# Sums of the activation blocks right behind their transposes, and act transposed on VectorE and through memory, in a hybrid decoder layer

## The chip, the cores and the metric

The kernel runs on one core of a Trainium2 chip. The metric is the device time of one execution in microseconds (us). The engines are named as in the profile: PE (TensorE, matrix products), PEld (its weight loads), DVE (VectorE), ACT (ScalarE), POOL (GpSimd), SP (SyncE, which issues nearly all transfers). SBUF is the on-chip memory, PSUM the banks that PE writes to.

## What is computed

One decoder layer in float32, 256 tokens, width 2048, inner width 5632 of the feed-forward part. The change touches the second half alone: the end of the mixer, the norm behind it and the feed-forward part. Cut to that, with the mixer's output as `mix`:

```python
mix = jnp.einsum('bse,ed->bsd', mix, w_out[l])
x = x + rmsnorm(mix, norm_post_mix[l])
h = rmsnorm(x, norm_pre_ffn[l])
g = jnp.einsum('bsd,df->bsf', h, w_gate[l])
up = jnp.einsum('bsd,df->bsf', h, w_up[l])
f = jnp.einsum('bsf,fd->bsd', jax.nn.silu(g) * up, w_down[l])
x = x + rmsnorm(f, norm_post_ffn[l])
```

## The kernel before

Every product is made of three passes: an operand is split into a rounded part h and a rest l, and PE sums h·h, l·h and h·l. ACT casts a weight tile w (128x2048) to wh (L185, for the pairs below L920), DVE forms wl = w − wh (L186, L921).

The program's order is written out by hand. A list holds steps, each of 12 matmuls on 128x512, for one of two blocks of 128 tokens (tb=0, 1). At each step the stream first resumes the side jobs whose time has come (`yield n` in a job means: go on n steps later), then splits the weight tile four places ahead, issues the next loads on SP as slots come free (three for w, two for raw), and then writes the step's matmuls. Each engine runs its instructions in that order. One instruction that waits holds up all behind it on its engine, and SP likewise.

The mixer's last chunk ends in `residual(tb)` (L747-802): it makes x, transposes it on PE, and writes H2, the split operand of gate and up. For tb=1 it ends with `form_sums` (L726) and `split_sums` (L741), the sums and differences S of H2's blocks that the pairs need.

The feed-forward part runs over 11 column blocks f of 512, in four parts: f=0-2, 3-5, 6-8, 9-10. f=0 has a plain chunk for gate and one for up (`post_gate` L822, `post_up` L831). Every later f is a `Pair`, which computes half of gate and up by seven products over sums of blocks (s1 to s7) and the rest plainly (g0, g1, u0, u1); the steps of u0 and u1 of f fill in between those of the pair of f+1, or in front of the down chunks when f ends a part:

```python
return (s[1] + fill[0] + s[7] + s[6] + fill[1] + s[5] + s[2] + s[3] + g[0] + g[1] + s[4])
```

s7 accumulates in the bank b7, which the pair before frees with its gate add for tb=1 (`gate`, L1006). Behind s5, ACT copies the bank to s (L1023) and s3 waits for this copy.

When u1 of f is done, sg holds act, tokens on partitions. `act_put` (L1037; for f=0 the end of `post_up`) turns it, 8 PE transposes of 128x128 into PSUM (tile ft), from where ACT casts h (L208) and DVE subtracts l (L209) into the tile act, the operand of the down products. After each part the down chunks n=0-3 run (L1079-1094): for each n, over the part's k tiles (one for each f), two steps each; a step on the k of f needs act of f.

Tiles named M come from a pool of three buffers of 128x1024: sg, v, s and others share it.

Of the kernel before, what the change touches and what calls it, by code (L numbers as in the profile page):

```python
# [25 lines left out]
F32 = mybir.dt.float32  # L26
# [34 lines left out]
def hybrid_layer_kernel(ctx: ExitStack, tc: tile.TileContext, x, xt, pack, lamv,  # L61
# [25 lines left out]
    def v3(ap, n):  # L87
        return ap.rearrange("p (a b) -> p a b", a=n)
# [637 lines left out]
    def form_sums():  # L726

        r = v3(T("sums"), 4)
        h, l = H2.part(1)
        for tb in range(2):  # L730
            tok = slice(tb * P, (tb + 1) * P)

            nc.vector.tensor_tensor(out=r[:, 2 * tb:2 * tb + 2].rearrange("p a (k t) -> p (a k) t", k=4),
                                    in0=h[:, :, tok].bitcast(F32), in1=l[:, :, tok].bitcast(F32),
                                    op=ALU.add)
        for o, a, b, op in [(3, 2, 3, ALU.add), (2, 0, 2, ALU.subtract), (0, 3, 0, ALU.subtract),
                            (1, 1, 0, ALU.subtract)]:
            nc.vector.tensor_tensor(out=r[:, o], in0=r[:, a], in1=r[:, b], op=op)
        return r

    def split_sums(r):  # L741
        sh, sl = v3(T("sumh", F32R), 4), v3(T("suml", F32R), 4)
        nc.scalar.copy(sh, r)
        nc.vector.tensor_tensor(out=sl, in0=r, in1=sh.bitcast(F32), op=ALU.subtract)
        st_["S"] = [t.rearrange("p s (k t) -> p s k t", k=4) for t in (sh, sl)]

    def residual(tb, bank):  # L747
        xr, mg = st_["x", tb], st_["mixg", tb]
        tok = slice(tb * P, (tb + 1) * P)
        square_into(bank, part[:, tb, 3:4])  # L750
        if tb:
            yield 1
        nc.vector.tensor_tensor(out=mg[:, 3 * C:], in0=bank, in1=st_["gpost"][:, 3 * C:],
                                op=ALU.mult)
        r = partial_rstd(part, tb, "rpost")

        def x2(n):
            c = slice(n * C, (n + 1) * C)
            nc.vector.scalar_tensor_tensor(out=xr[:, c], in0=mg[:, c], scalar=r[:, 0:1],
                                           in1=xr[:, c], op0=ALU.mult, op1=ALU.add)  # L760

        def tr(n):
            bk = aux_bank("ht")
            for j in range(4):
                nc.tensor.transpose(bk[:, j * P:(j + 1) * P],
                                    xr[:, n * C + j * P:n * C + (j + 1) * P], ident)
            for eng in range(2):
                for j in range(4):
                    k = n * 4 + j
                    g = pk[:, PK_GFFN + k:PK_GFFN + k + 1]  # L770
                    h, l = H2.at(k, 1, tok)
                    b = bk[:, j * P:(j + 1) * P]
                    if eng == 0:
                        nc.scalar.activation(h[:, 0], b, ACTF.Copy, scale=g)
                    else:
                        nc.vector.scalar_tensor_tensor(out=l[:, 0], in0=b, scalar=g,
                                                       in1=h[:, 0].bitcast(F32), op0=ALU.mult,
                                                       op1=ALU.subtract)

        x2(0)  # L780
        yield 1
        x2(1)
        x2(2)
        yield 1
        x2(3)
        tr(0)
        for n in range(1, 4):
            yield 1
            tr(n)
        yield 3  # L790
        for n in range(4):
            square_into(xr[:, n * C:(n + 1) * C], part2[:, tb, n:n + 1])
        yield 1
        rstd2[tb] = partial_rstd(part2, tb, "rffn")

        nc.sync.dma_start(xd[tb], xr)
        st_["x", tb] = None
        if tb:
            yield 1
            r = form_sums()  # L800
            yield 2
            split_sums(r)

    oc = []
    need = {0: [lambda: st_["av", 0]], 4: [lambda: st_["av", 1]],
# [16 lines left out]
    def post_gate(f, bank):  # L822
        while rstd2[0] is None or rstd2[1] is None:
            yield 1
        sg = v3(M("sg"), 2)
        st_["sg", f] = sg
        for tb in range(2):
            nc.scalar.activation(sg[:, tb], bank[tb], ACTF.Silu, scale=rstd2[tb][:, 0:1])
        st_["gate", f] = True

    def post_up(f, A, k, bank):  # L831
        while ("gate", f) not in st_:
            yield 1
        sg = st_["sg", f]
        for tb in range(2):
            nc.vector.scalar_tensor_tensor(out=sg[:, tb], in0=bank[tb], scalar=rstd2[tb][:, 0:1],
                                           in1=sg[:, tb], op0=ALU.mult, op1=ALU.mult)
            dve[0] += 0.6
        yield 2
        for tb in range(2):  # L840
            bk = aux_bank("ft")
            for j in range(4):
                nc.tensor.transpose(bk[:, j * P:(j + 1) * P], sg[:, tb, j * P:(j + 1) * P], ident)
            A.put_psum(k, 4, slice(tb * P, (tb + 1) * P), v3(bk, 4))

    def down_evac(pi, last, n, tb, bank):
        c = slice(n * C, (n + 1) * C)
# [39 lines left out]
    class Act:  # L887
# [9 lines left out]
            t = self.t[f]  # L897
            return t[:, 0, k % 4:k % 4 + n, tok], t[:, 1, k % 4:k % 4 + n, tok]

        put_psum = Operand.put_psum  # L900

    class Slot:

# [22 lines left out]
    class Pair:  # L926
# [88 lines left out]
        def after(self, what, tb):  # L1015
            if what == 1:
                self.v = v3(M("v"), 2)
                nc.scalar.copy(self.v[:, 0], self.b1)
            elif what == 6:
                nc.scalar.copy(self.v[:, 1], self.b1)  # L1020
            elif what == 5:
                self.s = M("s")[:, :C]
                nc.scalar.copy(self.s, self.b1)  # L1023
                nc.vector.tensor_tensor(out=self.s, in0=self.b7, in1=self.s, op=ALU.add)
            elif what == "g1" and tb == 0:
                self.sg = v3(M("sg"), 2)
                spawn(self.gate(0, self.b2, self.v[:, 0])).run()
            elif what == 4:
                spawn(self.gate(1, self.b7, self.v[:, 1])).run()
            elif what == "u1" and tb == 0:  # L1030
                self.up(0, self.b1)
            elif what == "u1":
                nc.vector.tensor_tensor(out=self.s, in0=self.b8, in1=self.s, op=ALU.add)
                self.up(1, self.s)
                st_["act", self.f] = spawn(act_put(self.A, self.k, self.sg), 3)

    def act_put(A, k, sg):  # L1037
        for tb in range(2):
            bk = aux_bank("ft")
            for j in range(4):  # L1040
                nc.tensor.transpose(bk[:, j * P:(j + 1) * P], sg[:, tb, j * P:(j + 1) * P], ident)  # L1041
            A.put_psum(k, 4, slice(tb * P, (tb + 1) * P), v3(bk, 4))
        yield 1

    def reload():
        load_gain(1, "gpf")
# [6 lines left out]
    for pi, (f0, f1) in enumerate(parts):  # L1053
        A = Act()
        last = pi == len(parts) - 1
        needs = {}
        for f in range(f0, f1):
            k = (f - f0) * 4
            needs[k] = [lambda f=f: st_["act", f]]
            if f:  # L1060
                pair = Pair(f, A, k)
                put(pair.steps(fill))
                fill = pair.up_steps()
                continue
            c = both(lambda bank, f=f: post_gate(f, bank))(Chunk("gate", H2))
            add(c, w_tiles(w_gate, 0, [(f * C, C)], 0, KT), stagger=True)

            def hook(bank, f=f, A=A, k=k):
                j = Job(post_up(f, A, k, bank), now[0])
                st_["act", f] = j  # L1070
                side.append(j)
            c = Chunk("up", H2)
            c.done = lambda tb, c=c, hook=hook: hook(c.bank) if c.left == [0, 0] else None
            st = steps_of(c, w_tiles(w_up, 0, [(f * C, C)], 0, KT))
            put(st[:4])
            fill = [st[4:6], st[6:]]
        put(fill[0] + fill[1])
        nk = (f1 - f0) * 4
        for n in range(4):  # L1079
            c = Chunk("down", A, needs=needs)  # L1080
            ts = w_tiles(w_down, f0 * C, [(n * C, C)], 0, nk)
            if last and n == 0:
                ts[0][1].post.append(reload)
            if last and n == 3:
                c.done = lambda tb, c=c, pi=pi: spawn(finish(pi, tb, c.bank[tb]))
                add(c, ts, stagger=True)
                continue
            both(lambda bank, pi=pi, last=last, n=n: post_down(pi, last, n, bank))(c)
            st = steps_of(c, ts)
            if n == 3:  # L1090
                put(st[:-4])
                fill = [st[-4:-2], st[-2:]]
            else:
                put(st)
# [82 lines left out]
```

## Time and profile before

| | |
|---|---|
| time, median of three runs | 1080.97 us (1080.56 to 1081.28) |
| the profiled execution: time, span | 1080.65 us, 1078.9 us |
| PE busy, share of the span, instructions | 1052.6 us, 98%, 4766 |
| DVE | 823.2 us, 76%, 858 |
| ACT | 562.4 us, 52%, 586 |
| transfers of queue q1: MB, share of 16 engines' span | 213.21 MB, 57.7% |
| the chain that ended last | PE 84%, DVE 8%, ACT 3%, DMA 2%, issue 2% |

The rows further down come from several views of one profiled execution. A busy PE isn't PE at its peak: the rows with PEclk give the clock that it was granted, 1.00 being 2.4 GHz and 0.50 being 1.2 GHz. A matmul's own duration (390 ns for 128x512) is longer than the distance from one to the next, since they overlap; a step of 12 takes 2.72 us from start to start. The idle time of an engine matters only where someone waits for it.

### The profile page before, as it was taken

To read this page: it belongs to the slowest core of one execution; us is meant where nothing else is said; L and a number is where in the kernel's file an instruction comes from. 1 tells how busy PE (TensorE), PEld (TensorE's weight loads), DVE (VectorE), ACT (ScalarE), POOL (GpSimd) and SP (SyncE) were. 2 spreads that over 40 slices of the span, in tenths; PEclk is the share of its full clock that TensorE was granted. 3 is DMA by queue.
4 is the path that set the end of the run, shared out by engine and by line. 5 is a ranking of instruction groups with operands and counts; after the bars stand their busy time and mean duration, and the time that the engine had idled before them with its cause. 6 is when DMAs were issued, how large, how long until landed. Compare 5 with 4: busy or idle time off the path is not lost.

```text
span 1078.9 us, 12015 instructions
## 1 busy us (share of the span) xinstructions
PE 1052.6 (98%) x4766; PEld 866.3 (80%) x4766; DVE 823.2 (76%) x858; ACT 562.4 (52%) x586; POOL 10.8 (1%) x16
## 2 busy tenths in 40 slices
PE   9999999999999979999999999999999999999986
PEld 7778888888888858888888887888888788888865
DVE  6589989898656888875578987567898855789655
ACT  6764564655645654654454655335465533446441
POOL 0000000001000000000000000000000000000000
PEclk9999999999999989999999999999999999999989
DMA  9876555444766627277354827745473684453922
GB/s 309 291 271 197 193 157 195 156 156 156 271 199 233 199 105 279 78 273 262 128 195 156 294 97 256 257 150 195 156 255 121 231 290 156 154 197 131 354 100 78
DMA packets 114265, 213.97 MB, mean 198 GB/s; under 512 B 4089, under 2 KB 23841, under 8 KB 112929
## 3 DMA queue, kind: packets, MB, share of 16 engines
q1 hardware_dynamic: 114208, 213.21, 57.7%
q8 instruction: 37, 0.61, 0.2%
q14 instruction: 20, 0.16, 0.0%
HBM read 208.99 MB, written 4.21 MB: 198 GB/s over the span
## 4 chain that ended last, share of the span: by engine, by line
PE 84%; DVE 8%; ACT 3%; DMA 2%; issue 2%; POOL 1%; SPq 0%; DVEq 0%; POOLq 0%; ACTq 0%
PE b L999 23%; PE mm L259 15%; PE mm L260 15%; PE mm L262 15%; PE b L1002 11%; DVE wl L186 2%; DVE wl L921 2%; ACT wh L185 2%; DMA w<-in_w_in_dram 1%; DVE w L954 1%; PE ft L1041 1%; DVE conv_acc L442 1%; DMA rb<-in_rel_bias_dram 1%; ACT wh L920 1%; PE scmm L262 1%
## 5 line engine op out<-in xcount | busy, mean ns | idle before, releaser
L186 DVE TENSOR_TENSOR wl<-w,wh 128x2048 fp32r<-128x2048 f32 (+1 forms) x160 | 340.6, 2130 | 130.4 <-ACT wh L185 126.8
L185 ACT CAST wh<-w 128x2048 fp32r<-128x2048 f32 (+1 forms) x160 | 285.0, 1783 | 186.8 <-PE mm L260 92.8
L999 PE MATMUL b<-wh,h2h 128*128 128x512 f32 x440 | 171.9, 391 | 0.0
L1002 PE MATMUL b<-wh,h2l 128*128 128x512 f32 x440 | 171.3, 389 | 0.0
L259 PE MATMUL mm<-wh,act 128*128 128x512 f32 x352 | 138.5, 393 | 2.5 <-ACT act L208 2.5
L260 PE MATMUL mm<-wh,act 128*128 128x512 f32 x352 | 138.2, 393 | 1.6 <-DVE act L209 1.6
L259 PE MATMUL mm<-wh,xh 128*128 128x512 f32 x320 | 128.0, 400 | 0.9 <-ACT wh L185 0.9
L260 PE MATMUL mm<-wh,xl 128*128 128x512 f32 x320 | 125.2, 391 | 0.0
L921 DVE TENSOR_TENSOR wl<-w,wh 128x2048 fp32r<-128x2048 f32 x40 | 91.6, 2289 | 38.1 <-ACT wh L920 37.3
L999 PE MATMUL b<-wl,h2h 128*128 128x512 f32 x440 | 117.7, 389 | 0.0
L920 ACT CAST wh<-w 128x2048 fp32r<-128x2048 f32 x40 | 76.5, 1912 | 73.0 <-DVE w L954 42.6
L999 PEld LDWEIGHTS b<-wl,h2h 128*128 128x128 f32 x440 | 82.6, 188 | 17.2
L999 PEld LDWEIGHTS b<-wh,h2h 128*128 128x128 f32 x440 | 82.6, 188 | 17.0
L1002 PEld LDWEIGHTS b<-wh,h2l 128*128 128x128 f32 x440 | 82.7, 188 | 16.9
L262 PE MATMUL mm<-wl,act 128*128 128x512 f32 x352 | 94.6, 391 | 0.0
L442 DVE SCALAR_TENSOR_TENSOR conv_acc<-conv_in,pk,conv_acc 128x255 f32<-128x255 f32 (+14 forms) x240 | 94.4, 467 | 0.0
L921 DVE TENSOR_TENSOR wl<-raw,wh 128x2048 fp32r<-128x2048 f32 x30 | 68.2, 2290 | 26.0 <-ACT wh L920 26.0
L262 PE MATMUL mm<-wl,xh 128*128 128x512 f32 x320 | 87.4, 391 | 0.2 <-DVE wl L186 0.2
L920 ACT CAST wh<-raw 128x2048 fp32r<-128x2048 f32 x30 | 57.4, 1913 | 50.6 <-DVE raw L954 45.9
L259 PEld LDWEIGHTS mm<-wh,act 128*128 128x128 f32 x352 | 66.6, 189 | 16.4 <-ACT act L208 2.7
L260 PEld LDWEIGHTS mm<-wh,act 128*128 128x128 f32 x352 | 66.6, 189 | 15.9 <-DVE act L209 2.2
L262 PEld LDWEIGHTS mm<-wl,act 128*128 128x128 f32 x352 | 66.5, 189 | 14.0
(170 smaller groups left out, 1293.4 us busy)
## 6 DMA issues: line engine op xcount, KB each, us to landing
w<-in_w_down_dram SPq DMA_DIRECT2D x44, 1024.0 KB, 5.0
w<-in_w_gate_dram SPq DMA_DIRECT2D x34, 1024.0 KB, 5.2
w<-in_w_in_dram SPq DMA_DIRECT2D x24, 1024.0 KB, 5.1
w<-in_w_up_dram SPq DMA_DIRECT2D x24, 1024.0 KB, 5.2
raw<-in_w_up_dram SPq DMA_DIRECT2D x20, 1024.0 KB, 8.2
w<-in_w_out_dram SPq DMA_DIRECT2D x16, 1024.0 KB, 5.0
w<-in_w_in_dram SPq DMA_DIRECT2D x24, 512.0 KB, 4.9
raw<-in_w_gate_dram SPq DMA_DIRECT2D x10, 1024.0 KB, 8.2
```

Of the source, the lines that this page charges most:

```text
L185: nc.scalar.copy(self.h[:, a:b], self.w[:, a:b])
L186: nc.vector.tensor_tensor(out=self.l[:, a:b], in0=self.w[:, a:b], in1=self.h[:, a:b].bitcast(F32), op=ALU.subtract)
L259: nc.tensor.matmul(bank, lhsT=h, rhs=t.h[:, j], start=first, stop=False)
L260: nc.tensor.matmul(bank, lhsT=l, rhs=t.h[:, j], start=False, stop=False)
L262: nc.tensor.matmul(bank, lhsT=h, rhs=t.l[:, j], start=False, stop=last)
L442: return lambda: nc.vector.scalar_tensor_tensor(out=conv_acc[:, cb, s:], in0=conv_in[:, cb, :S - s], scalar=w, in1=conv_acc[:, cb, s:], op ...
L920: nc.scalar.copy(self.h, w)
L921: nc.vector.tensor_tensor(out=self.l, in0=w, in1=self.h.bitcast(F32), op=ALU.subtract)
L954: nc.vector.tensor_tensor(out=out.w, in0=a.w, in1=b.w, op=ALU.subtract)
L999: nc.tensor.matmul(bank, lhsT=h[:, j], rhs=rhs, start=start and pas == 0 and j == 0, stop=stop and pas == 1 and j == SPLIT - 1, skip_group ...
L1002: nc.tensor.matmul(bank, lhsT=l[:, j], rhs=rhs, start=False, stop=False, skip_group_check=True)
L1041: nc.tensor.transpose(bk[:, j * P:(j + 1) * P], sg[:, tb, j * P:(j + 1) * P], ident)
```

## The change

Three things change. (1) In `residual(tb=1)` the sums are formed and split one and two steps behind the last transposes, ahead of the squares that give the norm's factor; `post_gate` starts a step later. (2) `act_put` no longer uses PE. DVE transposes sg in blocks of 32x32 into a tile sgt, SP writes sgt to memory (actd, 512 KB), two steps later SP reads it back in eight transfers of 64 KB (runs of 512 bytes) that put the blocks in their places in the tile actr, and two steps later ACT casts and DVE subtracts from actr (`put`). The job starts without the delay of three steps. (3) In each part's down chunks the last k tile of n=0 moves behind the other k tiles of n=1.

```diff
--- before.py
+++ after.py
@@ -787,7 +787,13 @@
         for n in range(1, 4):
             yield 1
             tr(n)
-        yield 3
+        if tb:
+            yield 1
+            r = form_sums()
+            yield 1
+            split_sums(r)
+        else:
+            yield 3
         for n in range(4):
             square_into(xr[:, n * C:(n + 1) * C], part2[:, tb, n:n + 1])
         yield 1
@@ -795,11 +801,6 @@
 
         nc.sync.dma_start(xd[tb], xr)
         st_["x", tb] = None
-        if tb:
-            yield 1
-            r = form_sums()
-            yield 2
-            split_sums(r)
 
     oc = []
     need = {0: [lambda: st_["av", 0]], 4: [lambda: st_["av", 1]],
@@ -822,6 +823,7 @@
     def post_gate(f, bank):
         while rstd2[0] is None or rstd2[1] is None:
             yield 1
+        yield 1
         sg = v3(M("sg"), 2)
         st_["sg", f] = sg
         for tb in range(2):
@@ -836,12 +838,7 @@
             nc.vector.scalar_tensor_tensor(out=sg[:, tb], in0=bank[tb], scalar=rstd2[tb][:, 0:1],
                                            in1=sg[:, tb], op0=ALU.mult, op1=ALU.mult)
             dve[0] += 0.6
-        yield 2
-        for tb in range(2):
-            bk = aux_bank("ft")
-            for j in range(4):
-                nc.tensor.transpose(bk[:, j * P:(j + 1) * P], sg[:, tb, j * P:(j + 1) * P], ident)
-            A.put_psum(k, 4, slice(tb * P, (tb + 1) * P), v3(bk, 4))
+        yield from act_put(A, k, sg)
 
     def down_evac(pi, last, n, tb, bank):
         c = slice(n * C, (n + 1) * C)
@@ -897,7 +894,14 @@
             t = self.t[f]
             return t[:, 0, k % 4:k % 4 + n, tok], t[:, 1, k % 4:k % 4 + n, tok]
 
-        put_psum = Operand.put_psum
+        def put(self, k, raw):
+
+            for tb in range(2):
+                r = raw[:, tb * C:(tb + 1) * C].rearrange("p (i k c) -> p k i c", i=4, k=4)
+                h, l = (t.rearrange("p k (i c) -> p k i c", i=4)
+                        for t in self.at(k, 4, slice(tb * P, (tb + 1) * P)))
+                nc.scalar.copy(h, r)
+                nc.vector.tensor_tensor(out=l, in0=r, in1=h.bitcast(F32), op=ALU.subtract)
 
     class Slot:
 
@@ -1032,15 +1036,32 @@
             elif what == "u1":
                 nc.vector.tensor_tensor(out=self.s, in0=self.b8, in1=self.s, op=ALU.add)
                 self.up(1, self.s)
-                st_["act", self.f] = spawn(act_put(self.A, self.k, self.sg), 3)
+                st_["act", self.f] = spawn(act_put(self.A, self.k, self.sg))
 
     def act_put(A, k, sg):
-        for tb in range(2):
-            bk = aux_bank("ft")
-            for j in range(4):
-                nc.tensor.transpose(bk[:, j * P:(j + 1) * P], sg[:, tb, j * P:(j + 1) * P], ident)
-            A.put_psum(k, 4, slice(tb * P, (tb + 1) * P), v3(bk, 4))
+
+
+        m = M("sgt")
+        for tb in range(2):
+            nc.vector.transpose(
+                out=m[:, tb * C:(tb + 1) * C].rearrange("p (u j c) -> p j u c", u=4, j=4),
+                in_=sg[:, tb].rearrange("p (j u c) -> p j u c", j=4, u=4))
         yield 1
+
+        d = dram.tile([P, 2 * C], F32, tag="actd", bufs=4, name="actd")
+        nc.sync.dma_start(d, m)
+        yield 2
+        a = d[:]
+        raw = M("actr")
+
+        for u in range(4):
+            for tb in range(2):
+                nc.sync.dma_start(
+                    raw[u * 32:(u + 1) * 32, tb * C:(tb + 1) * C].rearrange("p (i x) -> p i x", i=4),
+                    bass.AP(a.tensor, a.offset + tb * C + u * P,
+                            [[2 * C, 32], [32 * 2 * C, 4], [1, P]]))
+        yield 2
+        A.put(k, raw)
 
     def reload():
         load_gain(1, "gpf")
@@ -1087,7 +1108,12 @@
                 continue
             both(lambda bank, pi=pi, last=last, n=n: post_down(pi, last, n, bank))(c)
             st = steps_of(c, ts)
-            if n == 3:
+            if n == 0:
+
+                st0 = st
+            elif n == 1:
+                put(st0[:-2] + st[:-2] + st0[-2:] + st[-2:])
+            elif n == 3:
                 put(st[:-4])
                 fill = [st[-4:-2], st[-2:]]
             else:
```

What the order of instructions becomes is shown at three places. First DVE at the end of the mixer and in the first pair (sums, sumh, suml are the sums and their parts; prt and rs belong to the norm's factor), from right behind the split that follows H2's last blocks. Before:

```order
L921 TENSOR_TENSOR wl<-w,wh 128x2048
L954 TENSOR_TENSOR w<-raw,w 128x2048
L186 TENSOR_TENSOR wl<-w,wh 128x2048
L954 TENSOR_TENSOR raw<-raw 128x2048
L688 TENSOR_REDUCE prt<-part_90 128x1
L101 TENSOR_SCALAR rs<-prt 128x1
L921 TENSOR_TENSOR wl<-raw,wh 128x2048
L954 TENSOR_TENSOR w<-raw,w 128x2048
L733 TENSOR_TENSOR sums<-h2h_2787,h2l_2788 128x1024 x2
L738 TENSOR_TENSOR sums<-sums 128x512 x4
L921 TENSOR_TENSOR wl<-w,wh 128x2048
L744 TENSOR_TENSOR suml<-sums,sumh 128x2048
```

After:

```order
L733 TENSOR_TENSOR sums<-h2h_2787,h2l_2788 128x1024 x2
L738 TENSOR_TENSOR sums<-sums 128x512 x4
L925 TENSOR_TENSOR wl<-w,wh 128x2048
L958 TENSOR_TENSOR w<-raw,w 128x2048
L744 TENSOR_TENSOR suml<-sums,sumh 128x2048
L186 TENSOR_TENSOR wl<-w,wh 128x2048
L958 TENSOR_TENSOR raw<-raw 128x2048
L688 TENSOR_REDUCE prt<-part_90 128x1
L101 TENSOR_SCALAR rs<-prt 128x1
L925 TENSOR_TENSOR wl<-raw,wh 128x2048
```

The sums moved to the head of the list, and suml from its end to behind one split and one difference; the norm's factor (prt, rs) now stands behind them.

Second, DVE in pair 4, from the end of u1 of f=3 (the operation that writes sg from s) to the gate add (into sg from the bank b and v). Before:

```order
L1012 SCALAR_TENSOR_TENSOR sg<-s,rffn_3053,sg 128x512
L186 TENSOR_TENSOR wl<-w,wh 128x2048
L1024 TENSOR_TENSOR s<-b_3158,s 128x512
L186 TENSOR_TENSOR wl<-w,wh 128x2048
L921 TENSOR_TENSOR wl<-w,wh 128x2048
L209 TENSOR_TENSOR act<-ft,act 128x4x128 x2
L921 TENSOR_TENSOR wl<-w,wh 128x2048
L954 TENSOR_TENSOR w<-raw,w 128x2048
L186 TENSOR_TENSOR wl<-w,wh 128x2048
L954 TENSOR_TENSOR raw<-raw 128x2048
L1006 TENSOR_TENSOR sg<-b_4459,v 128x512
```

After:

```order
L1016 SCALAR_TENSOR_TENSOR sg<-s,rffn_3052,sg 128x512
L1046 STREAM_TRANSPOSE sgt<-sg 128x4x4x32 x2
L186 TENSOR_TENSOR wl<-w,wh 128x2048
L1028 TENSOR_TENSOR s<-b_3158,s 128x512
L186 TENSOR_TENSOR wl<-w,wh 128x2048
L925 TENSOR_TENSOR wl<-w,wh 128x2048 x2
L958 TENSOR_TENSOR w<-raw,w 128x2048
L904 TENSOR_TENSOR act<-actr,act 128x4x128 x2
L186 TENSOR_TENSOR wl<-w,wh 128x2048
L958 TENSOR_TENSOR raw<-raw 128x2048
L1010 TENSOR_TENSOR sg<-b_4476,v 128x512
```

The two block transposes stand at the head, and the two act subtractions moved from ahead of the fourth split to ahead of the fifth, right behind the difference w<-raw,w; the splits and the gate add behind them keep their order.

Third, SP's queue in the same place (every load of a tile is one row of L165; here + is what the change adds):

```order
 L165 DMA raw<-in_w_gate_dram 128x4x512
 L165 DMA w<-in_w_gate_dram 128x4x512 x2
 L165 DMA raw<-in_w_up_dram 128x4x512 x2
 L165 DMA w<-in_w_gate_dram 128x4x512
+L1052 DMA actd<-sgt 128x1024
 L165 DMA w<-in_w_up_dram 128x4x512 x2
+L1059 DMA actr<-actd 32x4x128 x8
 L165 DMA raw<-in_w_gate_dram 128x4x512
 L165 DMA w<-in_w_gate_dram 128x4x512 x2
```

The write stands right behind a load of w_gate, and the eight reads behind the next two loads of w_up; on ACT (not shown) the two casts of act stand ahead of the cast of the tile whose split is the fifth in the list before.

## Rows read from the trace of the kernel before

**Rows 1.** Waits of PE: engine, line and releaser; total us, times, longest.

```profile
PE b L999 <- ACT sumh L743: 4.8, 1, 4.8
PE mm L259 <- ACT act L208: 2.5, 1, 2.5
PE b L1002 <- DVE suml L744: 1.9, 1, 1.9
PE mm L260 <- DVE act L209: 1.6, 1, 1.6
PE b L999 <- ACT s L1023: 1.5, 2, 0.8
```

**Rows 2.** Groups by line, PE: busy us, mean ns | idle before.

```profile
L1041 PE MATMUL ft<-ident,sg 128*128 128x128 f32 x80 | 10.4, 273 | 0.0
```

**Rows 3.** Windows: length, busy of PE, PEld, DVE, ACT, POOL; PEclk, DMA share, GB/s.

```profile
396.20:403.10 6.90, 4.99 (x12) 3.71 (x12) 6.58 (x3) 4.54 (x3) 0.00 (x0) 0.51 0.17 42
...
1020.00:1025.00 5.00, 5.00 (x25) 4.13 (x25) 3.00 (x3) 0.41 (x1) 0.00 (x0) 1.00 1.02 385
1027.70:1034.50 6.80, 4.75 (x10) 3.43 (x11) 3.40 (x3) 0.84 (x2) 0.00 (x0) 0.50 0.68 235
```

**Rows 4.** Timeline, DVE, around the sums: start, duration, engine, line, operation.

```profile
369.66 2.28 DVE L186 TENSOR_TENSOR wl<-w,wh 128x2048 fp32r<-128x2048 f32 x1
...
388.71 2.35 DVE L733 TENSOR_TENSOR sums<-h2h,h2l 128x1024 f32<-128x1024 f32 x2
391.10 2.87 DVE L738 TENSOR_TENSOR sums<-sums 128x512 f32<-128x512 f32 x4
```

**Rows 5.** Timeline from pair 4 to pair 5, in order of time, three engines.

```profile
606.45 2.28 DVE L186 TENSOR_TENSOR wl<-w,wh 128x2048 fp32r<-128x2048 f32 x1
...
618.10 1.92 ACT L185 CAST wh<-w 128x2048 fp32r<-128x2048 f32 x1 [2.15 <-DMA w<-in_w_up_dram]
...
620.51 2.28 DVE L186 TENSOR_TENSOR wl<-w,wh 128x2048 fp32r<-128x2048 f32 x1
...
631.47 0.69 DVE L1006 TENSOR_TENSOR sg<-b,v 128x512 f32<-128x512 f32 x1
...
631.89 1.07 PE L999 MATMUL b<-wl,h2h 128*128 128x512 f32 x4
...
649.99 0.50 PE L999 MATMUL b<-wh,sumh 128*128 128x512 f32 x1 [0.71 <-ACT s L1023]
```

**Rows 6.** Timeline of SP's queue, then transfers: count, KB each, us to landing.

```profile
608.76 0.37 SPq L165 DMA_DIRECT2D w<-in_w_gate_dram  x1
...
613.76 0.37 SPq L165 DMA_DIRECT2D w<-in_w_up_dram  x1
...
w<-in_w_gate_dram SPq DMA_DIRECT2D x1, 1024.0 KB, 5.2
...
w<-in_w_up_dram SPq DMA_DIRECT2D x1, 1024.0 KB, 6.9
...
xr<-in_xt_dram SPq DMA_DIRECT2D x2, 128.0 KB, 2.8
...
out_dram<-xres SPq DMA_DIRECT2D x8, 256.0 KB, 2.2
```

**Rows 7.** Timeline from pair 1 to pair 2, SP's queue, DVE and PE.

```profile
416.61 0.37 SPq L165 DMA_DIRECT2D w<-in_w_gate_dram  x1
...
428.66 2.28 DVE L186 TENSOR_TENSOR wl<-w,wh 128x2048 fp32r<-128x2048 f32 x1
...
439.61 0.69 DVE L1006 TENSOR_TENSOR sg<-b,v 128x512 f32<-128x512 f32 x1
...
457.64 1.07 PE L999 MATMUL b<-wl,h2h 128*128 128x512 f32 x4
```

**Rows 8.** Last down part: load issued at 1023.07, then PE's third tile.

```profile
w<-in_w_down_dram SPq DMA_DIRECT2D x1, 1024.0 KB, 7.9
...
1042.31 1.07 PE L262 MATMUL mm<-wl,act 128*128 128x512 f32 x4
```

## The prediction

> **What bounds the kernel now.** I read three views in this order. The page's first part gives TensorE (PE) 1052.6 of 1078.9 us, 98% of the span, and the chain that ended last is 84% PE: a microsecond taken from PE's own work is a microsecond gained, as long as no other engine becomes late. The view of PE's waits says how near the others are: the longest wait is 4.8 us, for the sums of H2, then 2.5 us for the act blocks in the last down part; the copy of s costs 1.5 us in two places [rows 1]. So the cover is thin. The timeline then tells where: VectorE (DVE) has long operations in a fixed order, 2.28 us for each split of a weight tile, and PE meets it at the pair boundaries with less than a microsecond in hand. Those boundaries decide this change. One more thing is to be seen: after its two long waits PE ran for 6.8 to 6.9 us at a granted clock of 0.50 to 0.51 (the level of 1.2 GHz), while elsewhere it is 1.00 [rows 3]. Such a stretch does half the work of its length, so each costs 3.4 us beside the wait itself.
>
> **The transposes of act leave PE.** 80 of them take 10.4 us [rows 2], and 8 in the gate/up chunk another 1.04 us: 11.4 us in all, 1.04 us for each of the 11 f. It is returned only where PE sets the end. In their place DVE gets two 128x512 block transposes, which the trace of before doesn't show. The nearest row is a DVE operation on 128x512, 0.69 us [rows 5], or 0.72 from the four of the sums [rows 4]; the bounds are 0.5 (the row's bytes with one input fewer, an estimate) and 1.4 each (twice the row), and I take 0.7, 1.4 us for an f.
>
> A transpose of 128x128 costs PE 273 ns here at four bytes [rows 2] and the DVE pair 1.4 us against PE's 1.04 by my estimate. The Trainium skill, "VectorE: DVE Perf Modes", section "The three transpose paths", has 390 ns for TensorE and 311 ns for VectorE at two bytes, and says that VectorE transposes blocks of 32x32 alone; its "Rules for kernel authors" advise TensorE for a whole 128x128. By its ratio the pair would be 0.8 us instead of 1.4; and by its rule the blocks have to be put in place by something else, which is what the trip through memory does.
>
> **The trip through memory.** The built program shows where its instructions stand. On SP's queue the write of 512 KB stands right behind the w_gate load, then come two w_up loads, each of which waits for a DVE split, and only then the eight reads of 64 KB; the first read waits for the write to land, and the seventh and eighth wait for the landing of the first and second w_up load, whose semaphores they take over. On ACT the two casts of act stand ahead of the cast wh (L185) of the next tile; on DVE the two act subtracts stand ahead of the split wl (L186). Behind that split stand the raw subtraction and gate add (L1006, after: L1010), and this add must be done before PE may start step s7 of the next pair in its bank. So when the eighth read is late, two queues and then PE are late with it. This chain exists for f=0, 3 and 6, whose pair is followed by another pair.
>
> Part 1 in numbers. Before, DVE's split before the w_gate load ends at 606.45+2.28=608.73 [rows 5] and the load is issued at 608.76 [rows 6]; the DVE transposes ahead of it make that 610.1, and 5.2 us for the load [rows 6] 615.4. The write follows at the queues' rate, 385 GB/s [rows 3], 1.4 us: 616.8. The second w_up load was issued at 613.76 and took 6.9 us, so it landed at 620.66 [rows 6]; with 512 KB more ahead of it and the shift I take 622.4. The eighth read then needs its issue, 0.4 to 0.5, and its transfer. Nearest rows: 2.8 us for 128 KB into SBUF and 2.2 for the 256 KB stores at the end, 5.2 for a whole tile [rows 6]; I take 2.8 (the same direction). Act is in SBUF at L=625.6; the bounds are 623.3 (the load lands as before, transfer 2.2) and 628.1 (transfer 5.2). Then ACT casts act (0.6, as its copies of 128x512 take) and the weight (1.92, before at 618.10), and DVE's split starts at 628.1 instead of 620.51: 7.6 us late [rows 5]. The gate add ended at 631.47+0.69=632.16 and will end at 639.75. PE is through with the step before s7 at 631.89+1.07=632.96, in the new kernel 1.04 us sooner, at 631.9: it idles 7.8 us, where before it had no wait at all. An idle of this length was followed by the low clock in both places seen [rows 3]: 3.4 us. The six steps up to s3 take 16.3 us at 2.72 each, so s3 starts at 639.75+3.4+16.3=659.5 instead of 649.99 [rows 5]: +9.5, and -1.04 for the transposes of f=4 behind it. **Part 1: +8.5.** Part 2 has the same order and the same wait before s3 (the two of 1.5 us in [rows 1]): **+8.5.** No stall needs L of 617.7 or less, that is, act landed before the wh cast starts at 618.10; that is 5.6 us below the lower bound of L.
>
> The Trainium skill, "DMA: Bandwidth & Descriptors", section "Anatomy of one DMA", gives for transfers issued by GpSimd 2.0 us fixed and bytes over 436 GB/s; by it a read would be 2.15 us, and the sum 2 us lower in all (three times 0.65). Its "Specifications" say that pieces of 512 bytes still run at full rate; the reads' pieces are just that long, so by the page they need no extra. The 256 KB stores at 2.2 us are below its 2.6.
>
> Part 0 by the same steps. The w_gate load is issued at 416.61, L is 431.6 (15 us later, as 625.6 is behind 610.1), the split starts at 434.1 instead of 428.66 (+5.45), the gate add ends at 445.75 instead of 440.30 [rows 7]. Before, 457.64+1.07-440.30=18.4 us lay between its end and that of s2; after, 16.3+3.4=19.7: 465.5 instead of 458.71. **Part 0: +6.8-1.04=+5.7.**
>
> **The sums earlier.** Before, form_sums runs at 388.71 and takes 2.35+2.87 us, and PE waits 4.8+1.9 us for what follows from it. After, it stands behind the split that starts at 369.66, so the sums are ready at 371.9+5.2=377.1, and DVE's four splits and subtractions that stood ahead move behind [rows 1, 4]. DVE's work is the same, only sorted by need: the last operand of s6 comes at 400.4 and s6 ends near 401.3 instead of 406.1. Part of that goes again, because DVE reaches the copy of s 2 us later and has the block transposes ahead of it: s3 of pair 1 starts about 3 us earlier. These 3 us end in the wait of part 0, whose start is set by DMA and DVE, so they add nothing to the sum.
>
> **The other f.** In f=1, 4, 7 the reads come in the down chunk, with some 2 us in hand: no stall, -1.04 each, counted above. f=9 costs 1.4-1.04=+0.4. f=2, 5, 8 run inside down chunks with much slack: -3.1.
>
> **The last down part.** The last k-tile of chunk 0 moves behind those of chunk 1, which gives act of f=10 two more steps, 5.4 us; before, PE waited 2.5+1.6 us there [rows 1] and three tiles were done at 1042.31+1.07=1043.38 [rows 8]. But the write stands behind a w_down load that took 7.9 us [rows 8]: it lands at about 1032.5, the reads at about 1038, act is split at 1041, and PE is out of other work at 1030.05. The three tiles end at 1046 to 1047.7: **+3.5** (0 to +7).
>
> **Sum.** 5.7+8.5+8.5+0.4-3.1+3.5=+23.5. The profiled execution took 1080.65, 0.3 below the median; so 1080.65+23.5=1104, whichever of the two is taken.
>
> **Rivals.** *The read-back is hidden.* The price is decided at one place: whether act is in SBUF when ACT would cast the next weight (617.7 in part 1). It would be, if the reads didn't wait for the w_up loads and went in between their packets. Then the gate add is at most 0.4 us late; part 0 gives -1.0, parts 1 and 2 -0.6 each, the rest as above: 1080.65-1.0-1.2+0.4-3.1+3.5=1079. For it speaks that DMA was busy only 57.7% of the span; against it the order on SP. Not slower, at chance 0.10. *PE alone counts.* DVE and ACT have slack everywhere and all of PE's relief arrives: -11.4, -4.8 at the sums, -7.5 in the last part (2.5+1.6 of waits and 3.4 of low clock): 1057. The 98% speak for it, the 0.8 us in hand at the pair boundary (632.16 against 632.96) against it: 0.08. *The reads are much slower* than a row of whole tiles, because of their short pieces, and take 7.9 us like the slow tile of [rows 8] instead of 2.8: L is 5.1 us later at three places, 1104+15=1119, and more where the raw load queued behind the reads is late too: 0.10.
>
> **How the numbers follow.** The forecast has 0.72. Its lower end: L at its lower bound, 3 times -2.3, the last part at 0, and one of the low-clock stretches left out: 1104-6.9-3.5-3.4=1090; its upper end, with transfers at 5.2 us and the last part at +7: 1104+7.5+3.5=1115. The range for 8 in 10 goes on to 1079 (half of the hidden case) and to 1120. What a measurement can tell from no change is about 0.2%, 2.2 us. Faster: 0.08 and 0.04 of the hidden case, 0.12. Same: 0.06 of it. Slower: 0.72+0.10=0.82.
>
> **What would show it.** PE's waits: three of some 6 to 8 us at s7 of pairs 2, 5 and 8 for the gate add, each followed by a stretch at half clock, and no 4.8 us for sumh. ACT's waits: its act cast waiting for the actr reads. If those reads land before the weight's cast, the forecast is wrong. If DVE's block transposes take well over 0.7 us, the DVE chain is later still; if the eighth read doesn't wait for the w_up load, L falls by some 4 us.

## The result: slower by 5.6%, two and a half times as much as forecast

The changed kernel takes 1141.1 us (median of four runs, 1138.8 to 1142.9), the kernel before 1080.8 in the same comparison: a ratio of 1.0558, 95% interval 1.0533 to 1.0583. The forecast was 1104, its range ended at 1120. The direction was right, and so was the mechanism that it named, act read back late. But it put that mechanism at four places (three pairs and the last down part), and it acts at seven.

The page of the changed kernel (its execution of 1138.8 us, the fastest of the four): its span, busy times, and the chain that ended last.

```profile
span 1137.0 us, 12040 instructions
## 1 busy us (share of the span) xinstructions
PE 1055.9 (93%) x4678; PEld 861.1 (76%) x4678; DVE 836.1 (74%) x880; ACT 561.5 (49%) x586; POOL 10.8 (1%) x16
...
PE 52%; DVE 16%; DMA 16%; ACT 7%; issue 5%; SPq 3%; POOL 1%; DVEq 0%; ACTq 0%; POOLq 0%
```

PE has 88 instructions fewer, as it should, and its share of the chain that ended last fell from 84% to 52%; DVE and DMA have 16% each. PE isn't the bound any more in long stretches. Its waits say where (total us, times, longest):

```profile
PE mm L259 <- ACT act L903: 35.2, 4, 16.0
PE b L1003 <- DVE sg L1010: 16.5, 3, 5.5
PE b L1003 <- ACT s L1027: 6.6, 7, 1.3
PE b L1003 <- ACT v L1022: 3.5, 1, 3.5
PE b L1003 <- ACT wh L185: 2.9, 3, 1.7
```

Beside [rows 1]: the wait for sumh (4.8) is gone. The three waits for the gate add (L1010) are those that were forecast at the starts of pairs 2, 5 and 8. Of the first line, 35.2 us for act in the down chunks, the forecast had the wait in the last part (16.0) alone; the other 19.2 are at f=2, 5 and 8, for which it had "much slack".

PE computes the same steps in the same number in both kernels, only without the transposes, so the start of each step can be set against its start before. This table gives the lag at the ends of the forecast's own terms (from the timelines of PE; the terms add up, but for rounding, to the whole 58.0 by which PE is late at the end). A term for act of f=2, 5 or 8 begins behind the third down step, where PE's transposes of that f stood before, so that what is saved there counts in it, as in the forecast.

| term of the sum | lag at its end, us | measured | forecast |
|---|---|---|---|
| part 0 with the sums, to the third down step | +5.6 | +5.6 | +5.7 |
| act of f=2 in the down chunks | +13.3 | +7.7 | -1.0 |
| part 1 (pairs 4 and 5), to the third down step | +23.5 | +10.1 | +8.5 |
| act of f=5 | +30.0 | +6.5 | -1.0 |
| part 2 (pairs 7 and 8), to the third down step | +38.5 | +8.5 | +8.5 |
| act of f=8 | +46.5 | +8.0 | -1.0 |
| pair 10 | +46.8 | +0.3 | +0.4 |
| the last down part | +58.0 | +11.2 | +3.5 |

Four terms were within 1.6 us. Three had the wrong sign, and one was forecast at a third of its size.

**Where the 7.7 us at f=2 come from.** SP's queue of the changed kernel in the down chunks of part 0 (start, duration of the issues, count):

```profile
502.56 1.05 SPq L165 DMA_DIRECT2D raw<-in_w_up_dram  x2
503.65 0.73 SPq L1052 DMA_DIRECT2D actd<-sgt  x1
504.48 0.45 SPq L165 DMA_DIRECT2D w<-in_w_down_dram  x1
514.70 3.84 SPq L1059 DMA_DIRECT2D actr<-actd  x8
```

and the transfers issued between 500 and 505 (count, KB each, us to landing):

```profile
w<-in_w_down_dram SPq DMA_DIRECT2D x2, 1024.0 KB, 13.7
raw<-in_w_up_dram SPq DMA_DIRECT2D x2, 1024.0 KB, 9.3
actd<-sgt SPq DMA_DIRECT2D x1, 512.0 KB, 11.0
```

Then what DVE, ACT and PE did in the same stretch:

```profile
498.64 1.30 DVE L1046 STREAM_TRANSPOSE sgt<-sg 128x512 f32<-128x512 f32 x2
...
520.23 1.14 ACT L903 CAST act<-actr 128x512 fp32r<-128x512 f32 x2 [15.86 <-DMA actr<-actd]
...
520.90 0.80 PE L259 MATMUL mm<-wh,act 128*128 128x512 f32 x1 [6.70 <-ACT act L903]
```

The block transposes are done at 499.9. The write waits for SP until 503.65 (SP stood until 502.1 for the split that frees a slot for a w_down load), stands behind that load and two raw loads of 1 MB, and lands 11.0 us later. The first read can go only then, the eighth is issued at 518.5, and act is there at 520.2: 20 us after the transposes. The moved k tile gives PE eight down steps, 21.8 us, from the end of u1; they ran out at 514.2, and PE waits 6.7 us. The last part is the same with more in the way: the write is issued at 1076.99, 2.7 us behind the transposes, and takes 10 us, and PE waits 16.0.

Also new are seven waits of about 1 us for the copy of s, against two before. On ACT this copy waited for DVE's block transposes:

```profile
413.88 0.59 ACT L1027 COPY s<-b 128x512 f32<-128x512 f32 x1 [4.09 <-DVE sgt L1046]
```

### The profile page after: what moved, and what is told of

It reads as the page before. It is cut to its first block, busy times and chain, and to the rows that moved or that the text cites. A ratio compares the mean times of both kernels' runs of the same rounds, so it can differ in the third digit from the quotient of the medians.

```text
span 1137.0 us, 12040 instructions
## 1 busy us (share of the span) xinstructions
PE 1055.9 (93%) x4678; PEld 861.1 (76%) x4678; DVE 836.1 (74%) x880; ACT 561.5 (49%) x586; POOL 10.8 (1%) x16
## 4 chain that ended last, share of the span: by engine, by line
PE 52%; DVE 16%; DMA 16%; ACT 7%; issue 5%; SPq 3%; POOL 1%; DVEq 0%; ACTq 0%; POOLq 0%
PE mm L259 12%; PE mm L260 12%; PE mm L262 11%; PE b L1003 9%; DMA actd<-sgt 6%; DVE wl L186 5%; PE b L1006 4%; DVE wl L925 4%; ACT wh L185 4%; DMA actr<-actd 3%; DMA w<-in_w_in_dram 3%; DVE w L958 2%; DMA w<-in_w_down_dram 2%; SPq L1059 2%; ACT wh L924 2%
## 5 line engine op out<-in xcount | busy, mean ns | idle before, releaser
L259 PE MATMUL mm<-wh,act 128*128 128x512 f32 x352 | 141.1, 401 | 35.5 <-ACT act L903 35.2
L260 PE MATMUL mm<-wh,act 128*128 128x512 f32 x352 | 140.7, 400 | 0.0
L259 PEld LDWEIGHTS mm<-wh,act 128*128 128x128 f32 x352 | 68.2, 194 | 51.5 <-ACT act L903 36.9
L1003 PE MATMUL b<-wh,sumh 128*128 128x512 f32 x160 | 67.6, 422 | 26.6 <-DVE sg L1010 16.5
L260 PEld LDWEIGHTS mm<-wh,act 128*128 128x128 f32 x352 | 68.1, 193 | 16.0 <-DVE act L904 1.8
```

Of the source, the lines that this page charges most:

```text
L259: nc.tensor.matmul(bank, lhsT=h, rhs=t.h[:, j], start=first, stop=False)
L260: nc.tensor.matmul(bank, lhsT=l, rhs=t.h[:, j], start=False, stop=False)
L1003: nc.tensor.matmul(bank, lhsT=h[:, j], rhs=rhs, start=start and pas == 0 and j == 0, stop=stop and pas == 1 and j == SPLIT - 1, skip_group ...
```

## Experiments

The theories: A, the trip through memory costs nearly all, because its data come late; B, DVE's transposes and the new places in the queues of DVE and ACT cost by themselves; C, the moved sums or the moved k tile cost. Within A: Q, it is the place in SP's queue; L, it is the length of the trip wherever it is issued; S, it is not the data but SP standing still, or the traffic.

**The sums alone.** On the kernel before:

```diff
-        yield 3
+        if tb:
+            yield 1
+            r = form_sums()
+            yield 1
+            split_sums(r)
+        else:
+            yield 3
```

(their old place at the end of residual taken out, and the one step more in post_gate.)

> The kernel before with the sums' move alone. Theory A (the trip of act through memory costs nearly all of the 60 us; the sums help): PE is 2.6 us ahead at the end of pair 1, as in the changed kernel, and keeps 1.8 to 2.6 of it, since the gate add stands in its way by 0.8 us at most: 1078 to 1079 us. Theory C (the moved sums or the moved k tile cost time themselves): over 1081 us.

1079.0 us, ratio 0.9988 (0.9979 to 0.9998): A, at the edge of what can be told. PE is 3.5 us ahead at s7 of pair 1 and 1.8 two steps later, and keeps 1.6 of it to the last part.

**The moved k tile alone.**

```diff
+            if n == 0:
+                st0 = st
+            elif n == 1:
+                put(st0[:-2] + st[:-2] + st0[-2:] + st[-2:])
```

> The kernel before with the moved k tile of the down chunks alone. Theory A: the waits of 2.5 and 1.6 us in the last part go, and the low clock behind them with 3.4 us: 1073.5 us, nothing lost in the other parts. Theory C: over 1081 us, by waits for act or for down tiles at chunks 0 and 1 of parts 0 to 2.

1073.8 us, 0.9939 (0.9924 to 0.9954). As A has it: the two waits of [rows 1] in the last part are gone, with the low clock behind them.

**Both moves, with the PE transposes kept.**

> The kernel before with both moves, the PE transposes of act kept; the rest to the changed kernel is the turning of act alone. Theory A: the two gains add, 1071 us, so the new way of turning act costs some 70 us. Theory C: over 1081 us, and act's turning costs less than 60.

1071.8 us, 0.9921 (0.9906 to 0.9936). C is out: both moves help, and they add. The new way of turning act therefore costs 1141.1-1071.8=69 us, more than the whole result.

**No trip.** The changed kernel with act cast from the block transposes in SBUF:

```diff
-        d = dram.tile([P, 2 * C], F32, tag="actd", bufs=4, name="actd")
-        nc.sync.dma_start(d, m)
-        yield 2
...
-        yield 2
-        A.put(k, raw)
+        yield 4
+        A.put(k, m)
```

> The changed kernel without the write to memory and the reads; act is cast and split from the tile of block transposes, so the blocks stand in wrong places and the output is not the layer's. It leaves two block transposes on DVE, the casts and the subtractions, in the places that they had. Theory A (the trip's latency): no wait of PE for act is left, PE's 11.4 us are returned less some 2 us for DVE's transposes, beside what the two moves give: 1060 to 1064 us. Theory B (the block transposes and the act casts that stand ahead of weight casts cost by themselves): at least 1090 us, with waits for the gate add at the starts of pairs 2, 5 and 8.

1086.6 us, 1.0060 (1.0044 to 1.0077): 54.5 us less than with the trip, but neither theory's number. A is right that the trip is most of it, and wrong that without it PE's relief would show. PE's waits here:

```profile
PE b L1003 <- ACT s L1027: 11.8, 7, 2.4
PE b L1003 <- DVE sg L1010: 4.1, 3, 1.5
...
PE mm L260 <- DVE act L904: 1.9, 1, 1.9
PE mm L259 <- ACT act L903: 1.6, 1, 1.6
```

The gate add (B's place) is down to 4.1, but the copy of s costs 11.8. In the trace of this kernel ACT waits 34.6 us in seven places for the tile sgt before that copy. s doesn't read sgt; it shares the pool M with it, three buffers. By the program's order the buffer that s gets next is the one of sg, which the block transposes must have read.

**No trip, transposes into PSUM.** As the last, but (and the lines that use m changed to fit)

```diff
-        m = M("sgt")
+        m = [aux_bank("ft") for tb in range(2)]
```

> As e4_no_trip (no write, no reads, the output not the layer's), but DVE's block transposes write to the two PSUM banks that the PE transposes used, not to a tile of the pool M. Theory M (in e4_no_trip the 11.8 us of waits for the copy of s come from the pool of three M buffers: s gets the buffer of sg, which the late block transposes still read): these waits fall back to 1.5 to 2 us, and the time to 1072 to 1077 us. Theory D (DVE's 1.4 us more for each f delay the chain by themselves): the waits before s3 stay, 1084 us or more.

1077.6 us, 0.9978 (0.9969 to 0.9988): theory M, though 0.6 us above its 1072 to 1077; D asked for 1084 or more. PE's waits:

```profile
PE b L1003 <- DVE sg L1010: 7.6, 3, 2.7
...
PE b L1003 <- ACT s L1027: 2.2, 2, 1.1
```

The waits for s are back at two, 2.2 us. ACT's wait before this copy here:

```profile
ACT s L1027 <- DVE sg L1016: 22.0, 6, 4.0
```

ACT still stands there (34.6 us in e4_no_trip), but for the operation just ahead of the transposes, as it does four times in the kernel before. Without the trip the buffers are worth 9.0 us. What is left to e3_sums_down, 5.8 us, is for the transposes on DVE and the later act: the gate add is late by up to 2.7 us at three places, and act in the last part by 3.5 us with low clock behind it. PE's relief is in this number already.

**The trip issued by POOL.**

```diff
-        nc.sync.dma_start(d, m)
+        nc.gpsimd.dma_start(d, m)
-                nc.sync.dma_start(
+                nc.gpsimd.dma_start(
```

> The changed kernel with the write and the eight reads issued by POOL, which has nothing else to do there, instead of SP. Theory Q (the trip is slow because its transfers stand in SP's queue among the weight loads and the two raw loads): the write lands some 4 us and the reads some 8 us after the block transposes; the waits for act in the down chunks (35.2 us) and most of those for the gate add (16.5 us) go: 1085 to 1095 us. Theory L (the trip is long by itself, wherever it is issued): 1115 us or more.

1102.3 us, 1.0214 (1.0198 to 1.0231), between Q and L. Transfers and waits:

```profile
actd<-sgt POOLq DMA_DIRECT2D x11, 512.0 KB, 3.1
actr<-actd POOLq DMA_DIRECT2D x88, 64.0 KB, 6.6
```

```profile
PE b L1003 <- DVE sg L1010: 12.5, 3, 5.5
PE mm L259 <- ACT act L903: 11.1, 1, 11.1
PE b L1003 <- ACT s L1027: 5.8, 7, 1.4
```

The same write lands in 3.1 us instead of a median of 7.0, the reads are no faster. But POOL also issues the write earlier. At f=2:

```profile
495.99 0.56 POOL L1052 DMA_DIRECT2D actd<-sgt  x1 [23.91 <-DVE sgt L1046]
```

That is 0.3 us behind the block transposes and 2.3 us ahead of the raw loads; in the changed kernel it is 3.7 us behind the transposes and behind the raw loads. The three waits at f=2, 5, 8 are gone, so Q is right for them. At the pairs and in the last part (11.1) the trip is too long from either queue: L holds there. The other queue, with the earlier issue that comes with it, is worth 38.8 us; the two weren't tried apart.

**The raw loads behind the trip.**

```diff
-            while q and free[tag] and q[0][0] - i <= 9:
+            while q and free[tag] and q[0][0] - i <= (9 if tag == "w" else 7):
```

> The changed kernel with the raw loads issued up to two tiles later: in the down chunks of parts 0 to 2 the two raw w_up loads of 1 MB now stand behind the write and the reads of f=2, 5, 8 instead of ahead of the write; nearly all else keeps its order. Theory Q: the write there lands in 4 to 6 us instead of 11, act is in SBUF before PE asks for it, and the three waits of 5.4 to 7.0 us with the low clock behind them go: 1115 to 1120 us. Theory L: no more than 8 us gained, 1133 us or more.

1124.6 us, 1.0416 (1.0398 to 1.0433): 16.5 us gained. That is again between the two. The same stretch of SP and ACT as above:

```profile
501.68 0.50 SPq L1052 DMA_DIRECT2D actd<-sgt  x1
503.46 0.37 SPq L165 DMA_DIRECT2D w<-in_w_down_dram  x1
509.88 3.65 SPq L1059 DMA_DIRECT2D actr<-actd  x8
513.63 0.39 SPq L165 DMA_DIRECT2D w<-in_w_down_dram  x1
514.06 1.06 SPq L165 DMA_DIRECT2D raw<-in_w_up_dram  x2
```

```profile
514.69 1.16 ACT L903 CAST act<-actr 128x512 fp32r<-128x512 f32 x2 [11.18 <-DMA actr<-actd]
```

```profile
PE mm L259 <- ACT act L903: 22.6, 4, 16.6
PE b L1003 <- DVE sg L1010: 16.6, 3, 5.5
```

The first read goes at 509.9 instead of 514.7 and act is there at 514.7 instead of 520.2. PE waits 6.0 us at the three places in all, instead of 19.2; the other waits stay, as this edit leaves their order. So the raw loads are the cause of two thirds of those waits; the write still takes 8 us behind a w_down load.

**The trip made, but nobody waiting for it.** The reads go from memory to memory, act is cast from the block transposes:

```diff
-        raw = M("actr")
+        raw = dram.tile([P, 2 * C], F32, tag="actr", bufs=4, name="actr")
-        A.put(k, raw)
+        A.put(k, m)
```

> The changed kernel with the write and the reads in SP's queue as they are, but the reads go from memory to memory and act is made from the block transposes, as in e4_no_trip; so nothing waits for the trip but SP itself, and the output is not the layer's. Theory W (the trip costs because ACT, DVE and PE wait for its data): as e4_no_trip, 1086 to 1090 us. Theory S (it costs because SP stands waiting for the write ahead of the next loads, or because 11.5 MB more share the DMA engines): 1100 us or more, with waits for weight loads.

1088.0 us, 1.0072 (1.0057 to 1.0087), as without the trip (1.0044 to 1.0077). W holds and S is out: SP's waiting and the traffic cost nothing that can be told. The 54.5 us of the trip are PE, by way of ACT and DVE, waiting for the data.

**Two steps at the sums.** On e3_sums_down, once without the one step that post_gate waits more, and once with the norm's factor a step earlier:

```diff
-        yield 1
+        if not tb:
+            yield 1
         rstd2[tb] = partial_rstd(part2, tb, "rffn")
```

> e3_sums_down without the one step that the gate's silu starts later. If this step costs what PE shows for it in e3_sums_down (a wait of 1.0 us before the first step of pair 1 for the silu), PE is 1 us earlier there; what is left of it at the end is bounded by the gate add before s7 of pair 2, which has less than 1 us in hand: 1071 to 1072 us, no change beyond 0.2%.

> e3_sums_down with the norm's factor of tb=1 formed a step earlier, ahead of a split and a difference on DVE. In e3_sums_down ACT stands 5.3 us for this factor, with the cast for s7 and the copy of v behind it, and PE waits 3.5 us for the copy of v, with 1.7 us of low clock behind it. If that ACT wait is the cause, PE's wait of 3.5 us goes and PE is 4 to 5 us earlier at the end of pair 1. If the DVE chain to the gate add is set by the loads of w_up (as the prediction has it), PE gives this back in a new wait at s7 of pair 2 and the time stays at 1070.5 to 1072; if not, 1067 to 1068 us.

1071.5 us (0.9917, 0.9902 to 0.9932) and 1070.4 us (0.9909, 0.9893 to 0.9926). The first does nothing: the wait of 1.0 us for the silu is still there, so the step isn't its cause. The second took the wait for the copy of v from 3.5 to 2.5 us, less than thought, and PE moved about 1.2 us ahead by the traces; it gave none of it back at s7 of pair 2. In time that isn't clear of e3_sums_down. It is the fastest of the kernels run, with a ratio to the kernel before of 0.991.

## Why the prediction failed

**Right: which engine, and the chain in the pairs.** A late read-back holds ACT's casts, then DVE's split and the gate add, then PE at s7. In part 0, with the terms of the forecast beside the rows (act cast, split, gate add, PE at s7):

```profile
431.17 1.14 ACT L903 CAST act<-actr 128x512 fp32r<-128x512 f32 x2 [7.25 <-DMA actr<-actd]
...
434.15 2.29 DVE L186 TENSOR_TENSOR wl<-w,wh 128x2048 fp32r<-128x2048 f32 x1 [1.03 <-ACT wh L185]
...
445.11 0.68 DVE L1010 TENSOR_TENSOR sg<-b,v 128x512 f32<-128x512 f32 x1
...
445.94 0.77 PE L1003 MATMUL b<-wh,sumh 128*128 128x512 f32 x1 [5.52 <-DVE sg L1010]
```

Forecast: act there at 431.6, the split at 434.1, the end of the gate add at 445.75; beside [rows 7] each came true within half a microsecond. So did the reason: the eighth read waits for the landing of the second w_up load. SP's wait for it (between 414 and 432 us):

```profile
SPq L1059 <- DMA w<-in_w_up_dram: 2.5, 1, 2.5
```

s3 of pair 2 started at 464.94, against 465.5 forecast. Two errors cancel inside: the low clock behind the wait cost 1.6 us and not 3.4, and a wait of about 1 us for the copy of s came on top. Part 2 met its 8.5 in part by luck as well: PE waited 5.5 us for the gate add where 7.8 was forecast, the low clock cost 1.7, and waits of 1.2 us for the copy of s and 0.9 for the cast of a weight made up the rest.

**The step that failed: "f=2, 5, 8 run inside down chunks with much slack: -3.1".** It was said without a sum, while the same sum had been made for part 0 with care. The slack was there: 21.8 us of down steps. The trip took 20 us from the block transposes, which themselves begin 6 us after the end of u1, and PE asked 6.7 us too early. SP's order in the changed kernel shows the write behind two raw loads, and the raw loads' times to landing were on the page (8.2 us). The error is +22.3 measured against -3.1, 25 of the 34.5 us that the forecast missed. e8_raw_behind (16.5 us from moving the raw loads, the three waits down from 19.2 to 6.0) and e6_pool_queue (the three waits gone) show the cause. Right beside it: at f=1, 4 and 7, with "some 2 us in hand", PE has no wait for act.

**Mis-sized: the last part, +3.5 forecast, +11.2 measured.** The gain was counted right: at the second step behind the old waits PE is 7.1 us less late than before. Then it waits 16.0. The forecast let the write land 9.5 us after 1023, that is, at about 1079 by the changed kernel's lag; it was issued only at 1076.99, since SP first issued a w_down load that waits for a split which DVE makes after the block transposes, and it took 10 us behind three w_down loads that hadn't landed yet.

**Mis-sized: what leaves PE.** Eight transposes give back some 0.9 us and not 1.04: at nine places the lag falls by 0.8 to 0.95 for it, over the step behind them and the one after (the eight overlap the matmuls on either side). For 11 f that is an estimated 10 us instead of 11.4.

**Mis-sized: the low clock, 3.4 us for a wait.** The windows of [rows 3] don't bear it out: in both PE stood still a second time, and in that time the low clock costs nothing. The first one, in the kernel before (the wait for sumh, the second wait, the start of the next step):

```profile
395.95 0.57 PE L999 MATMUL b<-wh,sumh 128*128 128x512 f32 x1 [4.83 <-ACT sumh L743]
398.43 0.80 PE L1002 MATMUL b<-wh,suml 128*128 128x512 f32 x1 [1.91 <-DVE suml L744]
...
403.20 0.39 PE L999 MATMUL b<-wh,sumh 128*128 128x512 f32 x1
```

From start to start this step took 7.25 us instead of 2.72; less the second wait of 1.9 that is 2.6 us of low clock, and as much at 1028. e2_down agrees: 6.6 us gained, against waits of 2.5+1.6 and 2.6. Behind the seven long waits of the changed kernel (three for the gate add, four for act) it was 1.6 to 2.0 us six times, and 2.9 once (last section).

**Right: the price of the transposes on DVE.**

```profile
L1046 DVE STREAM_TRANSPOSE sgt<-sg 128x512 f32<-128x512 f32 x22 | 14.3, 689 | 0.2
```

0.69 us, as the nearest row; the two of an f take 1.3 us. The Trainium skill's ratio of 311 to 390 ns at two bytes ("VectorE: DVE Perf Modes", "The three transpose paths") would have made it an estimated 0.4 each: the trace disagrees at four bytes.

**Missed: the buffers of pool M.** The forecast saw the copy of s behind the transposes in pair 1 only. It is in seven places, and e4 and e5 price it at 9 us without the trip. Whether it costs as much beside the trip, where other waits overlap it, wasn't tried: PE's waits for s are 6.6 us there. Pair 10 shows it alone: its +0.3 is a wait of 1.3 us for the copy of s, less the 0.9 of the transposes, and the forecast's +0.4, 1.4 us of DVE less 1.04, met it by luck.

**Right for this kernel only: the sums' 3 us.** The forecast had them end in the wait at s7 of pair 2. In the changed kernel they do: PE is 3.1 us ahead through most of pair 1, and part 0 ends as forecast. The reason, that DVE's chain to the gate add is set by the loads, doesn't hold by itself: with the PE transposes 1.6 us stay to the last part in e1, 2.3 in e3, and e10 gave nothing back at s7. In the changed kernel it is the late read-back that holds the chain.

**Right: the last read.** The forecast took 2.8 us for it, with bounds of 2.2 and 5.2. The reads of the changed kernel (min, median, max us to landing), and the eighth of f=0 alone:

```profile
DMA to landing us min/median/max: 1.9/5.5/8.4
```

```profile
actr<-actd SPq DMA_DIRECT2D x1, 64.0 KB, 2.4
```

The eighth, which goes when the load ahead of it has landed, took 1.9 to 2.6 us at every f for which the trace has it; it is the one that ACT waits for. The median of 5.5 us comes from the seven ahead of it, which in the pairs stand behind the w_up loads and land before the eighth. So the rival of slow reads (7.9 us, because of short pieces) is out. An estimate by the Trainium skill's formula ("DMA: Bandwidth & Descriptors", "Anatomy of one DMA") gives 2.15 us. The page has it for transfers that GpSimd issues; the reads that POOL issued in e6_pool_queue took 3.8 us or more, with loads under way beside them.

## What to carry to other kernels

A step that goes through memory is priced from the transfers that stand ahead of it in its queue at each place where it stands, and compared with the consumer's distance at each: a place called slack without that sum was worth 25 us here. A new tile in a rotating pool changes who waits for whom among tiles that have nothing to do with it. And one edit that bundles three should be taken apart: two of the three were worth 0.8% together, and the third cost eight times as much.

## What the runs showed of the hardware

The same 512 KB write landed in 3.1 us (median) from POOL's queue and in 7.0 (up to 11.9) from SP's, at the same places in the program. What was already under way counted in both: in the last part POOL's write, issued behind weight loads of SP's queue, took 7.7 us too.

The low clock behind a wait isn't a fixed price. The windows behind the waits of 5.5 (pair 2), 6.7, 5.5 (pair 5) and 16.0 us (length, busy of PE, PEld, DVE, ACT, POOL, then PEclk):

```profile
445.90:452.70 6.80, 6.76 (x23) 5.53 (x24) 5.36 (x3) 6.80 (x6) 0.00 (x0) 0.77 0.01 2
520.90:527.70 6.80, 6.80 (x23) 5.25 (x24) 5.76 (x4) 4.66 (x4) 0.00 (x0) 0.76 0.43 151
654.80:661.60 6.80, 6.76 (x18) 5.36 (x19) 5.38 (x3) 6.80 (x6) 0.00 (x0) 0.57 0.00 1
1093.60:1100.40 6.80, 6.76 (x21) 5.11 (x22) 2.20 (x4) 1.23 (x3) 0.00 (x0) 0.71 0.01 2
```

Six of the seven waits have 0.71 to 0.77 behind them, a loss of 1.6 to 2.0 us over 6.8; pair 5 has 0.57, a loss of 2.9, behind a wait as long as that of pair 2. In both places of [rows 3], with a loss of 2.6 us, a second wait followed right behind the first matmul. A second wait isn't needed for so large a loss, since pair 5 has none behind it. What sets the size wasn't tried.
